# Output-product weights issued from GpSimd's queue in a two-layer hybrid attention trunk

## The chip, the cores and the metric

One core of one Trainium2 chip. The metric is the device time of one execution in microseconds; the median of several executions is given. The core's engines are TensorE (PE in the profile, its weight loads PEld), VectorE (DVE), ScalarE (ACT), GpSimd (POOL) and SyncE (SP), whose queue issues most transfers.

## The reference

Two layers over x of 256 rows and 1024 columns, and 256 rows of memory tokens, all in fp32:

```
for layer in range(2):
    h = rms_norm(x, norm_g[layer])
    sb_q, sb_k, sb_v, sb_g, mb_q, mb_k, mb_v, mb_g, mem_q, mem_g = split(h @ w_in[layer])   # 1024 x 3584
    o_sb  = stick_breaking_attention(sb_q, sb_k, sb_v) * silu(sb_g)        # 6 heads of 64
    o_mb  = causal_softmax_attention(rotary(mb_q), rotary(mb_k), mb_v) * silu(mb_g)   # 6 heads
    mk, mv = split(rms_norm(mem, mem_norm_g[layer]) @ w_mem_kv[layer])     # 1024 x 512
    o_mem = softmax_attention(mem_q, mk, mv) * silu(mem_g)                 # 4 heads
    x = x + concat(o_sb, o_mb, o_mem) @ w_out[layer]                       # 1024 x 1024
return rms_norm(x, final_norm_g)
```

With 256 rows the block-sparse attention of the reference has one block, so it is plain causal attention.

## The kernel before

**Precision.** Each weight chunk is loaded from DRAM into one of 7 buffers `raw` as fp32, then split into a high part (`hi_task`: a cast on ScalarE or VectorE) and a low part (`lo_task`: raw minus high, on VectorE); both go into one of 8 buffers `hl`. Activations are split in the same way (tiles `T`, `mxhi`, `mxlo`). Each product is three matmuls: high by high, low by high, high by low. For the pieces named in `DBL` the two with the same weights run as one 512-wide matmul and the two halves are added on VectorE afterwards.

**Chunks.** `ORDER` gives the weight pieces of each layer: column ranges of w_in, the two halves of w_mem_kv (mk, mv), and at each layer's end `wo0`, `wo1` and `wo2`, the three column ranges (384, 384 and 256) of w_out. A piece is cut into chunks of at most 768 columns by 128 rows; `KORD` is the order of w_out's eight row blocks, and only neighbouring blocks share a chunk. There are 114 chunks, 24 of them of w_out. When VectorE has made the low part of chunk j, `lo_task` issues the load of chunk j + 7 through `dma_chunk`, into the buffer that came free. All but the first two loads go out on SyncE's queue. `X_AT`, `CST_AT`, `X0_AT` and `X1_AT` say behind which chunk the transposed x, the constants and the two halves of x are loaded.

**Attention.** Head pairs of the kinds sb, mb and mem pass through `pair_scores` (matmuls on half of the array), softmax or the stick-breaking scan, `pair_turn` (32x32 transposes on VectorE into a tile `D`), a trip through DRAM, and `pair_task` (values, then the gate, then `mxhi` and `mxlo`). A trip (`trip`) is one write `Z<-D` and four reads (eight, of half the size, for the pairs in `HALVES`), into tiles shown as F, T, uT or ga. All are issued by SyncE in the same queue as the weight loads. `SCG` and `PVG` group the pairs whose scores or values go to TensorE together.

**Order.** The program is written by a planner while it is built: each stream of work is a generator, `Sched` estimates each engine's time from cost constants, and the next step is the one that can start first, by priority among steps that start within `SLACK`. All engines run their instructions in the order that comes out, each through its own queue; on a queue, an instruction that waits holds those behind it. The planner allows SyncE `RING` = 8 open transfers; it plans with the constants at the top of the file (`PRI`, the `P_` values, `HOLD`, `CROWD`, `DVE_HI` and so on). Helper lines in the profile: L261 all matmuls, L278 and L280 ScalarE's copies and activations, L284, L288, L292 and L299 VectorE's operations, L366 loads, L922 and L935 the write and reads of a trip, L486, L600 and L604 GpSimd's own DMAs (gains, and the rows of the norms).

Of the kernel before, what the change touches and what calls it, by code (L numbers as in the profile page):

```python
# [25 lines left out]
        "mem_q": (3072, 256), "mem_g": (3328, 256)}  # L26
LEAD = 8
RAW = 7
KORD = ((0, 1, 4, 5, 2, 3, 6, 7), (4, 5, 0, 1, 6, 7, 2, 3))
LAT_SAME, LAT_CROSS = 130.0, 240.0  # L30
PE_LATE = 375.1
NORM_LATE = 1029.7
DG_LATE = 885.3
COLD = 3900.0
PRI = {"sb": (-58, 4), "mb": (-198, -6), "mem": (30, 48)}
P_EV = 45
P_H0 = -22
P_RX = -136
P_M0 = 60
P_RM = -207  # L40
P_M1 = 44
URG = 1
X_AT = {4: 4, 5: 5, 8: 6, 10: 7}
CST_AT = 12
X0_AT = 15
X1_AT = 11
DMA_GBS = 330.0
RING = 8
SP_ISSUE = 450.0
POOL_ISSUE = 1000.0  # L50
# [2 lines left out]
DMA_GBS_1K = 285.0  # L53
TRIP_LAT = 1500.0
MEM_AT = 0
ORDER = (["sb_qk", "mb_k", "mb_q", "mv", "mk", "mb_g", "mem_q", "sb_v", "mb_v", "sb_g", "mem_g"], ["mv", "mk",
         "mb_q", "mb_k", "mem_q", "sb_q", "sb_k", "sb_v", "mem_g", "sb_g", "mb_g", "mb_v"])
NCH = {"sb": 3, "mb": 3, "mem": 2}
SILU = ((("sb", "mb"), ("mem",)), (("sb",), ("mb", "mem")))
TABLE = 1400.0  # L60
P_SILU = 12
SCG = (((("sb", 2), ("mem", 1), ("mb", 2)), (("mb", 1), ("mem", 0)), (("mb", 0),), (("sb", 0),), (("sb", 1),)),
       ((("mb", 0), ("sb", 2)), (("sb", 0), ("sb", 1)), (("mb", 2), ("mem", 0)), (("mem", 1),), (("mb", 1),)))
PVG = (((("mb", 1), ("mb", 0)), (("mem", 1), ("mem", 0)), (("sb", 1), ("mb", 2)), (("sb", 2),), (("sb", 0),)),
       ((("mem", 1), ("mb", 1)), (("sb", 0), ("sb", 1)), (("sb", 2), ("mb", 0)), (("mb", 2), ("mem", 0))))
HOLD = 522.1238552621808
HALVES = [("F", 0, "mem", 0), ("F", 1, "sb", 2)]
CROWD = 50
SPARE1 = 5
SPARE2 = 1  # L70
DBL = (("mb_g", 1), ("mem_g", 1), ("mk", 0), ("mk", 1), ("sb_g", 1), ("sb_k", 1), ("sb_q", 1))
DVE_W = -195.89999999999998
AHEAD = 15
DVE_HI = 1739.1999999999998
SLACK_PE = 150
SLACK = 55.400000000000006


def _free(ap):
# [22 lines left out]
class Sched:  # L102
# [63 lines left out]
    def _by_form(self, cands):  # L166
# [10 lines left out]
        for c in cands:  # L177
            f = form(c)
            if f != "full":
                first = self.held.setdefault(c[3], now)  # L180
                n = sum(form(x) == f for x in cands)
                if f == "row":
                    n = min(n, (len(self.res["bank"].items) - SPARE2) // 2)
                if n < c[3].req.get("crowd", CROWD) and now < first + HOLD:
                    continue
# [39 lines left out]
def hybrid_trunk(ctx: ExitStack, tc: tile.TileContext, x, mem, norm_g, w_in, w_mem_kv, w_out,  # L225
                 final_norm_g, xT, memT, gcols, consts, out):
    nc = tc.nc
# [3 lines left out]
    S = Sched()  # L231
# [133 lines left out]
    def dma(dst, src, name=None, q=None, now=0.0):  # L365
        (q or nc.sync).dma_start(dst, src)  # L366
        if q is None:
            S.T["sp"] = max(S.T["sp"], now, ring[-RING]) + SP_ISSUE
            now = max(now, S.T["sp"] - SP_ISSUE)
        t = queue(_free(dst) * 4 * dst.shape[0], dst.shape[-1] * 4, now)  # L370
        if q is None:
            ring.append(t)
        if name:
            S.ready[name] = t


    class Piece:
        def __init__(self, name, layer, src, width):
            self.name, self.layer, self.width, self.src = name, layer, width, src
            self.nk = CH // width  # L380
            self.kord = KORD[layer] if name[:2] == "wo" else tuple(range(KT))
            self.kmap = {}
# [7 lines left out]
    for l in range(DEPTH):  # L390
        wi = w_in[l].rearrange("(k p) c -> p k c", p=128)
        wm = w_mem_kv[l].rearrange("(k p) c -> p k c", p=128)
        wo = w_out[l].rearrange("(k p) c -> p k c", p=128)
        names = ORDER[l] + ["wo0", "wo1", "wo2"]
        for n in names:
# [27 lines left out]
    def dma_chunk(now=0.0, q=None):  # L423
        j = prog["dma"]
        if j >= len(chunks):
            return
        p, kk, c, w = chunks[j]
        n = len(kk)
        dma(raws[j % RAW][:, :n * w].rearrange("p (k c) -> p k c", c=w),
            p.src[:, kk[0]:kk[0] + n, c:c + w], ("raw", j), q, now)  # L430
        prog["dma"] += 1
        if j in X_AT:
            load_xT(X_AT[j], X_AT[j] + 1, now=now)
        for t, at in enumerate((X0_AT, X1_AT)):
            if j == at:
                dma(xs[:, t, :], x_r[:, t, :], ("x", t), now=now)
        if j == CST_AT:
            dma(cst, consts[:, 0:512], "cst", now=now)
            dma(S.res["w"].items[0][2][:, :256], consts[:, 512:768], "msk", now=now)
# [75 lines left out]
    def tr_k(p, X, c, acc, k):  # L515
        j, o = p.loc(k, c * 128)
        hi, lo = his[j % LEAD], los[j % LEAD]
        if (p.name, p.layer) in DBL:
            last = k == KT - 1
# [162 lines left out]
    def pair_scores(l, kind, c):  # L682


        group = [g for g in SCG[l] if (kind, c) in g][0]
        need = [(n, l, i) for k, i in group for n in QK[k]]
        _, sc = yield R("pe", need=["setup"] + need, alloc=["bank", "bank"],
                        spare=lambda: SPARE1 + 2 * (len(group) - 1) * (group not in begun),
                        spare2=SPARE2, form="row", crowd=CROWD if len(group) == 1 else 1)
        begun.append(group)  # L690
# [48 lines left out]
    def soft_head(l, h, kind):  # L739
# [31 lines left out]
        n = reg[1][1]  # L771
        e, _ = yield R(("act", 0.833 * n + 372.0), ("dve", 0.52 * n + 260.0 + DVE_W))
        for t, (r0, r1) in enumerate(reg):
# [27 lines left out]
    def pair_task(l, kind, c):  # L801
# [4 lines left out]
        k = HCOL[kind] // 128 + c  # L806
        group = [g for g in PVG[l] if (kind, c) in g][0]
        need = []
        for q, i in group:
            need += [("F", l, q, i), (VN[q], l)]  # L810
        _, (o,) = yield R("pe", alloc=["bank"], spare=lambda: 1 + (len(group) - 1) * ((l, group) not in begun), spare2=0,
                          form="col", crowd=1 if len(group) > 1 or kind == "mem" and c == 1 else CROWD, need=need)
        begun.append((l, group))
# [26 lines left out]
    def gate_evac(l, kind, c, acc):  # L840
        k = HCOL[kind] // 128 + c
        need = [("gm", l - 1, k)] if l else ["rx"]
        if (kind + "_g", l) in DBL:
            yield R("act", need=[n for n in need if n != "rx"])
# [20 lines left out]
    def silu_task(l, kinds):  # L865
# [7 lines left out]
        nc.scalar.preload_act_table_set("natural_log_exp_and_others")  # L873
        S.op("act", 2.0 * TABLE)
        for k in ks_:
# [42 lines left out]
    def trip(D, F, e, name, need=(), alloc=()):  # L918
# [13 lines left out]
        for j in range(4):  # L932
            for i0 in range(0, 4, 2 if name in HALVES else 4):
                i1 = i0 + (2 if name in HALVES else 4)
                nc.sync.dma_start(Fv[32 * j:32 * j + 32, i0:i1],  # L935
# [13 lines left out]
    def evac_T(l, name, c, acc, scale, rb, rneed):  # L949
        kind = {"sb_q": "sb", "sb_k": "sb", "mem_q": "mem", "mk": "mem"}[name]  # L950
        need = [("qkdone", l - 1, kind, h) for h in (2 * c, 2 * c + 1)] if l else []
        dst = (qs if name in ("sb_q", "mem_q") else ks)[kind][:, c, :]
        if ("sb_qk" if l == 0 and kind == "sb" else name, l) in DBL:
            sc = scale if rb is None else 1.0
# [79 lines left out]
    def main():  # L1034
# [7 lines left out]
        S.free("bank", acc)  # L1042
        scale_task(uT, ("xT",), 0, hT, ("h", 0), P_H0)
        for t in range(2):
            S.spawn(row_stats(2, t, xs[:, t, :], "x", rcx, rbx), P_RX)
        S.spawn(rows_done("x", "rx", rbx), P_RX)

        def mem_loads():
            load_memT(0)
            dma(gb, mem_r[:, 0, :], ("mem", 0), now=S.cur.t)  # L1050
            scale_task(uT, ("memT", 0), 16, mT, ("mT", 0), P_M0)
            S.spawn(rows_task(3, lambda t: gb, "mem", "rm", rcm, rbm), P_RM)

# [7 lines left out]
        for l in range(DEPTH):  # L1061
# [15 lines left out]
            def T_piece(n, X, nchunk, need, post):  # L1077
                p = pieces[n, l]
                for c in range(nchunk):
                    acc = yield from bank()  # L1080
                    yield from tr_unit(p, X, c, acc, need, c == nchunk - 1)
                    S.spawn(post(c, acc), P_EV, S.cur.t)

            def N_piece(n, X, need, post):
                p = pieces[n, l]
                for t in range(2):
                    acc = yield from bank()
                    yield from nat_unit(p, X, t, acc[:, :p.width], need)
                    S.spawn(post(t, acc), P_EV, S.cur.t)

# [5 lines left out]
            for kinds in SILU[l]:  # L1096
                S.spawn(silu_task(l, kinds), P_SILU)
            for h in range(SBH):
                S.spawn(scan_head(l, h), PRI["sb"][1] + h)
            for h in range(MEMH):  # L1100
                S.spawn(soft_head(l, h, "mem"), PRI["mem"][1] + h)
            for h in range(SBH):
                S.spawn(soft_head(l, h, "mb"), PRI["mb"][1] + h)
            for kind, n in (("sb", 3), ("mb", 3), ("mem", 2)):
                for c in range(n):
                    S.spawn(pair_scores(l, kind, c), PRI[kind][0] + 2)
                    S.spawn(pair_turn(l, kind, c), PRI[kind][0] + 1)
                    S.spawn(pair_task(l, kind, c), PRI[kind][0])
            if l == 0:
# [4 lines left out]
                for k in range(KT):  # L1114
                    if k < 4:
                        groups = [range(3), range(3, 6)] if k < 2 else [range(6)]
                        for g in groups:
# [3 lines left out]
                                     (los, 0, [("lo", j)])]  # L1121
                            dbl = ("sb_qk", 0) in DBL
                            if k and dbl:
# [13 lines left out]
                for c in range(6):  # L1137
                    S.spawn(evac_T(0, "sb_q" if c < 3 else "sb_k", c % 3, accs[c], 0.125 if c < 3 else 1.0, rbx, "rx"),
                            2, S.cur.t)
            for i, p in enumerate(ORDER[l]):  # L1140
                if l == 0 and i == MEM_AT:
                    mem_loads()
                if l == 0 and set(ORDER[0][i:]) <= {"mk", "mv"} and not late:
                    late.append(scale_task(uT, ("memT", 1), 24, hT, ("mT", 1), P_M1))
                if p == "sb_q" and l == 1:
# [17 lines left out]
                elif p == "mb_k":  # L1163
                    S.spawn(rope_turn(l, p), 2, S.cur.t)
                    yield from N_piece(p, hT, hneed, lambda t, acc: rope_task(
                        l, "mb_k", t, acc, rr_(t) if l == 0 else 1.0))
                if {"mk", "mv"} <= set(ORDER[l][:i + 1]) and not S.res["F%d" % l].items and l not in given:
                    given.add(l)
# [5 lines left out]
            if l == 0 and not late:  # L1174
                late.append(scale_task(uT, ("memT", 1), 24, hT, ("mT", 1), P_M1))

# [77 lines left out]
```

## Time and profile before

| | |
|---|---|
| median of 3 runs | 269.87 us (268.92 to 269.91) |
| the profiled execution | 269.51 us |
| its span, first to last instruction | 267.7 us |
| granted TensorE clock | 0.998 |
| DMA moved in all | 67.08 MB, 251 GB/s on the mean |

The span is what the rows of the profile add up to; the time of the execution is 1.8 us longer. Places in the span are given as us from its start. A row of a group of instructions names line, engine, operation, what it writes and reads (buffer numbers left out), shapes and count, then busy us and mean ns of one. A row of a wait names who waited, for whom, the sum in us, how often, and the longest.

### The profile page before, as it was taken

Reading aid. Unit: us, or ns where it says so; the run is one execution under the profiler, and the core shown is the slowest. Engines: PE = TensorE matmul, PEld = TensorE weight load, DVE = VectorE, ACT = ScalarE, POOL = GpSimd, SP = SyncE. Lnnn points to the kernel's source line nnn. Section 1 sums busy time; section 2 is a strip of 40 time slices with the busy share of each in tenths; the row PEclk is TensorE's granted clock in tenths of the full one; section 3 lists DMA queues with packets and bytes.
Section 4 is the critical chain, followed back from the end, with each engine's and each line's share of the span. In section 5 each row is a group of like instructions: output and inputs, shape, how many; then the busy total and the mean of one; then the engine's idle time right before and its main releaser. Section 6 shows DMA issues by size and latency. Waiting matters only on the chain.

```text
span 267.7 us, 5170 instructions
## 1 busy us (share of the span) xinstructions
PE 259.6 (97%) x1775; PEld 240.7 (90%) x1775; DVE 223.4 (83%) x517; ACT 187.3 (70%) x399; POOL 5.9 (2%) x18
## 2 busy tenths in 40 slices
PE   8999999999999999899999999999999999999991
PEld 4999999899999998798999999888998889989991
DVE  4696789889999999895899678689999999995382
ACT  4679888798599598771886446488778999912053
POOL 1000100200000000000000000000000000000000
PEclk9999999999999999999999999999999999999999
DMA  6999998969999899897498756857699989681004
GB/s 217 365 399 400 390 342 286 321 193 223 303 294 337 241 311 282 249 286 250 112 322 256 253 182 237 277 172 255 214 266 358 270 238 307 182 239 34 0 2 157
DMA packets 52042, 67.08 MB, mean 251 GB/s; under 512 B 4336, under 2 KB 47728, under 8 KB 52016
## 3 DMA queue, kind: packets, MB, share of 16 engines
q1 hardware_dynamic: 50928, 64.65, 77.0%
q0 software_dynamic: 512, 1.31, 1.9%
q10 hardware_dynamic: 576, 0.79, 0.9%
q8 instruction: 14, 0.23, 0.3%
q14 instruction: 12, 0.10, 0.1%
HBM read 57.29 MB, written 9.44 MB: 249 GB/s over the span
## 4 chain that ended last, share of the span: by engine, by line
PE 71%; DMA 15%; DVE 7%; ACT 3%; SPq 1%; issue 1%; DVEq 0%; ACTq 0%
PE bank L261 70%; DMA raw<-in_w_out_dram 4%; DMA raw<-in_w_in_dram 4%; DMA F<-Z 3%; DVE hl L284 2%; DMA ga<-Z 2%; DMA T<-Z 2%; ACT a L280 1%; DVE a L727 1%; DVE D L794 1%; SPq L366 1%; DVE w L292 1%; ACT hl L278 1%; PE bank L267 1%; SPq L935 1%
## 5 line engine op out<-in xcount | busy, mean ns | idle before, releaser
L284 DVE TENSOR_TENSOR hl<-raw,hl 128x768 fp32r<-128x768 f32 (+2 forms) x114 | 100.8, 897 | 10.6 <-ACT hl L278 9.7
L261 PE MATMUL bank<-T,hl 128*128 128x256 f32 (+1 forms) x720 | 106.2, 307 | 0.2 <-DVE hl L284 0.2
L261 PEld LDWEIGHTS bank<-T,hl 128*128 128x128 f32 x720 | 96.5, 190 | 8.9 <-issue 1.3
L278 ACT CAST hl<-raw 128x768 fp32r<-128x768 f32 (+2 forms) x107 | 83.0, 797 | 19.9 <-PE bank L261 11.0
L261 PE MATMUL bank<-hl,T 128*128 128x384 f32 (+1 forms) x480 | 80.2, 325 | 0.0
L261 PEld LDWEIGHTS bank<-hl,T 128*128 128x128 f32 x480 | 78.4, 188 | 0.6 <-issue 0.5
L261 PE MATMUL bank<-hl,mxhi 128*128 128x384 f32 (+1 forms) x192 | 45.5, 320 | 0.0
L261 PEld LDWEIGHTS bank<-hl,mxhi 128*128 128x128 f32 x192 | 33.3, 189 | 1.1 <-issue 1.1
L261 PE MATMUL bank<-hl,mxlo 128*128 128x384 f32 (+1 forms) x96 | 30.5, 318 | 0.0
L280 ACT ACTIVATE junk<-xs 128x384 bf16<-128x384 f32 (+2 forms) x15 | 8.0, 531 | 18.6 <-DVE xs L284 16.9
L794 DVE STREAM_TRANSPOSE D<-w 128x384 f32<-128x384 f32 (+1 forms) x32 | 19.2, 600 | 0.9 <-ACT w L280 0.9
L261 PEld LDWEIGHTS bank<-hl,mxlo 128*128 128x128 f32 x96 | 18.1, 189 | 0.2 <-DVE mxlo L284 0.2
L280 ACT ACTIVATE w<-w,st 128x256 f32<-128x256 f32 (+1 forms) x30 | 13.4, 458 | 3.6 <-DVE st L747 2.3
L727 DVE TENSOR_TENSOR_SCAN a<-a,a 128x256 f32<-128x256 f32 (+1 forms) x24 | 12.9, 538 | 1.1 <-ACT a L280 1.1
L280 ACT ACTIVATE T<-uT,gc 128x256 fp32r<-128x256 f32 x24 | 11.1, 501 | 2.1 <-DMA uT<-xT_dram 2.1
L284 DVE TENSOR_TENSOR xs<-bank,xs 128x384 f32<-128x384 f32 (+1 forms) x11 | 5.7, 520 | 7.6 <-PE bank L261 7.6
L280 ACT ACTIVATE a<-a 128x384 f32<-128x384 f32 x24 | 11.8, 525 | 0.1
L280 ACT ACTIVATE a<-bank 128x384 f32<-128x384 f32 x24 | 11.3, 485 | 0.6 <-DVE bank L284 0.5
L288 DVE SCALAR_TENSOR_TENSOR T<-uT,gc,T 128x256 fp32r<-128x256 f32 x24 | 11.4, 477 | 0.4 <-ACT T L280 0.4
L292 DVE TENSOR_SCALAR w<-w,st 128x256 f32<-128x256 f32 (+1 forms) x34 | 9.3, 317 | 0.0
L280 ACT ACTIVATE w<-bank,st 128x256 f32<-128x256 f32 x16 | 7.4, 472 | 2.8 <-DVE st L760 2.8
L284 DVE TENSOR_TENSOR ev<-bank,gT 128x256 f32<-128x256 f32 x16 | 6.4, 418 | 3.0 <-PE bank L261 3.0
(104 smaller groups left out, 211.1 us busy)
## 6 DMA issues: line engine op xcount, KB each, us to landing
raw<-in_w_in_dram SPq DMA_DIRECT2D x70, 384.0 KB, 5.1
Z<-D SPq DMA_DIRECT2D x16, 384.0 KB, 5.4
raw<-in_w_out_dram SPq DMA_DIRECT2D x16, 384.0 KB, 5.3
raw<-in_w_mem_kv_dram SPq DMA_DIRECT2D x8, 384.0 KB, 5.8
T<-Z SPq DMA_DIRECT2D x24, 96.0 KB, 4.9
uT<-memT_dram SPq DMA_DIRECT2D x8, 256.0 KB, 6.5
Z<-D SPq DMA_DIRECT2D x4, 512.0 KB, 5.9
raw<-in_w_out_dram SPq DMA_DIRECT2D x8, 256.0 KB, 3.8
```

Of the source, the lines that this page charges most:

```text
L261: nc.tensor.matmul(out, lhsT=lhsT, rhs=rhs, start=start, stop=stop, **kw)
L267: nc.tensor.transpose(out, in_, idt)
L278: nc.scalar.copy(out, in_)
L280: nc.scalar.activation(out, in_, func, **kw)
L284: nc.vector.tensor_tensor(out, a, b, op=op)
L288: nc.vector.scalar_tensor_tensor(out, a, s, b, op0=op0, op1=op1)
L292: nc.vector.tensor_scalar(out, a, s, None, op0=op)
L366: (q or nc.sync).dma_start(dst, src)
L727: nc.vector.tensor_tensor_scan(a[:, r0:r1], a[:, r0:r1], u[:, r0:r1], 0.0, OP.add, OP.add)
L794: nc.vector.transpose(o, w[:, :n * 128].rearrange("p (m j r) -> p m j r", j=4, r=32))
L935: nc.sync.dma_start(Fv[32 * j:32 * j + 32, i0:i1], Zv.rearrange("(i r) (j e) -> j r i e", i=4, j=4)[j, :, i0:i1])
```

## The change

The chunks of w_out are issued from GpSimd's queue, and the planner counts GpSimd's time for them. With it come new values of the planner's constants: the order of pieces in layer 1 and of its row blocks of w_out, the groups, priorities, the pieces in `DBL` (mem_g of layer 0 and mem_q of layer 1 are added), the places of the constants' and x's loads, and which trips are read in halves.

```
 LEAD = 8
 RAW = 7
-KORD = ((0, 1, 4, 5, 2, 3, 6, 7), (4, 5, 0, 1, 6, 7, 2, 3))
+KORD = ((0, 1, 4, 5, 2, 3, 6, 7), (0, 1, 4, 5, 6, 7, 2, 3))
...
-PRI = {"sb": (-58, 4), "mb": (-198, -6), "mem": (30, 48)}
-P_EV = 45
-P_H0 = -22
-P_RX = -136
-P_M0 = 60
-P_RM = -207
-P_M1 = 44
+PRI = {"sb": (-68, 4), "mb": (-222, -8), "mem": (-2, 18)}
+P_EV = 11
+P_H0 = -82
+P_RX = -192
+P_M0 = 38
+P_RM = -121
+P_M1 = 60
 URG = 1
-X_AT = {4: 4, 5: 5, 8: 6, 10: 7}
-CST_AT = 12
-X0_AT = 15
-X1_AT = 11
+X_AT = {5: 4, 6: 5, 7: 6, 10: 7}
+CST_AT = 6
+X0_AT = 14
+X1_AT = 13
...
-ORDER = (["sb_qk", "mb_k", "mb_q", "mv", "mk", "mb_g", "mem_q", "sb_v", "mb_v", "sb_g", "mem_g"], ["mv", "mk",
-         "mb_q", "mb_k", "mem_q", "sb_q", "sb_k", "sb_v", "mem_g", "sb_g", "mb_g", "mb_v"])
+ORDER = (["sb_qk", "mb_k", "mb_q", "mv", "mk", "mb_g", "mem_q", "sb_v", "mb_v", "sb_g", "mem_g"], ["mk", "mv",
+         "mb_q", "mb_k", "mem_q", "sb_k", "sb_q", "sb_v", "mem_g", "sb_g", "mb_g", "mb_v"])
...
-TABLE = 1400.0
-P_SILU = 12
-SCG = (((("sb", 2), ("mem", 1), ("mb", 2)), (("mb", 1), ("mem", 0)), (("mb", 0),), (("sb", 0),), (("sb", 1),)),
-       ((("mb", 0), ("sb", 2)), (("sb", 0), ("sb", 1)), (("mb", 2), ("mem", 0)), (("mem", 1),), (("mb", 1),)))
-PVG = (((("mb", 1), ("mb", 0)), (("mem", 1), ("mem", 0)), (("sb", 1), ("mb", 2)), (("sb", 2),), (("sb", 0),)),
-       ((("mem", 1), ("mb", 1)), (("sb", 0), ("sb", 1)), (("sb", 2), ("mb", 0)), (("mb", 2), ("mem", 0))))
-HOLD = 522.1238552621808
-HALVES = [("F", 0, "mem", 0), ("F", 1, "sb", 2)]
-CROWD = 50
+TABLE = 1290.0
+P_SILU = 16
+SCG = (((("sb", 1),), (("mem", 0), ("mb", 0), ("mb", 2)), (("sb", 2), ("mem", 1)), (("mb", 1),), (("sb", 0),)),
+       ((("mb", 0), ("sb", 2)), (("sb", 1), ("sb", 0)), (("mb", 1), ("mem", 1)), (("mb", 2),), (("mem", 0),)))
+PVG = (((("mem", 0), ("mem", 1)), (("sb", 1), ("mb", 2)), (("mb", 1), ("mb", 0)), (("sb", 2),), (("sb", 0),)),
+       ((("sb", 0), ("sb", 1)), (("sb", 2),), (("mem", 1), ("mb", 2), ("mem", 0), ("mb", 1)), (("mb", 0),)))
+HOLD = 652.654819077726
+HALVES = [("F", 0, "mem", 0), ("F", 0, "mem", 1)]
+CROWD = 46
 SPARE1 = 5
-SPARE2 = 1
-DBL = (("mb_g", 1), ("mem_g", 1), ("mk", 0), ("mk", 1), ("sb_g", 1), ("sb_k", 1), ("sb_q", 1))
-DVE_W = -195.89999999999998
-AHEAD = 15
-DVE_HI = 1739.1999999999998
-SLACK_PE = 150
-SLACK = 55.400000000000006
+SPARE2 = 0
+DBL = (("mb_g", 1), ("mem_g", 0), ("mem_g", 1), ("mem_q", 1), ("mk", 0), ("mk", 1), ("sb_g", 1), ("sb_k", 1),
+       ("sb_q", 1))
+DVE_W = -295.9
+AHEAD = 20
+DVE_HI = 1339.1999999999998
+SLACK_PE = 20
+SLACK = 65.4
...
         p, kk, c, w = chunks[j]
         n = len(kk)
+        if p.name[:2] == "wo":
+            q = nc.gpsimd
+            S.T["pool"] = max(S.T["pool"], now) + POOL_ISSUE
+            now = S.T["pool"]
         dma(raws[j % RAW][:, :n * w].rearrange("p (k c) -> p k c", c=w),
             p.src[:, kk[0]:kk[0] + n, c:c + w], ("raw", j), q, now)
```

## Prediction

> **What bounds the kernel now.** I read the page's first table, then the waits of TensorE, then busy time by stretches, then the chain that ended last.
>
> ```profile
> span 267.7 us, 5170 instructions
> PE 259.6 (97%) x1775; PEld 240.7 (90%) x1775; DVE 223.4 (83%) x517; ACT 187.3 (70%) x399; POOL 5.9 (2%) x18
> ```
>
> ```profile
> PE bank L261 <- DMA F<-Z: 1.0, 1, 1.0
> PE bank L261 <- DMA T<-Z: 0.3, 1, 0.3
> PE bank L261 <- DVE hl L284: 0.2, 1, 0.2
> ```
>
> TensorE is busy 259.6 of 267.7 us and idles behind other work for 1.5 us in all (besides the start of the program, before anything is loaded). So waits can give 1.5 us and no more; anything further must come out of TensorE's own instructions. Where the 1.5 us lies, the stretches show (busy us of PE, PEld, DVE, ACT, POOL in turn, instructions in brackets):
>
> ```profile
> 70.00:80.00 10.00, 10.00 (x72) 9.25 (x72) 10.00 (x44) 7.81 (x28) 0.00 (x0) 1.00 0.94 281
> 80.00:90.00 10.00, 10.00 (x67) 9.26 (x67) 10.00 (x23) 9.23 (x20) 0.00 (x0) 1.00 1.00 316
> 90.00:100.00 10.00, 10.00 (x86) 9.30 (x84) 9.10 (x27) 6.87 (x22) 0.00 (x0) 1.00 0.94 278
> 100.00:110.00 10.00, 8.76 (x79) 7.59 (x77) 9.57 (x25) 7.44 (x9) 0.00 (x0) 1.00 1.02 281
> 110.00:120.00 10.00, 10.00 (x62) 9.51 (x58) 9.44 (x18) 8.29 (x14) 0.00 (x0) 1.00 0.94 265
> ```
>
> TensorE loses 1.24 us between 100 and 110 us, the end of layer 0's attention. VectorE is nearly as full there: its idle time from 70 to 120 us is 0.90 + 0.43 + 0.56 = 1.9 us. So this stretch has two bounds, and TensorE's gap can close only as far as VectorE follows. The chain says what ended the gap:
>
> ```profile
> 97.86 5.54 DMA raw<-in_w_out_dram
> ...
> 104.25 5.25 DMA F<-Z
> 109.50 0.14 issue
> 109.64 28.08 PE bank L261 x189
> ...
> 145.52 116.71 PE bank L261 x751
> ```
>
> A w_out load (5.54 us) stands ahead of the read F<-Z (5.25 us) that TensorE waits for at 109.64. Behind that the chain is TensorE to its last matmul, 145.52 + 116.71 = 262.2 us: layer 1 has no wait, so nothing to gain there by queues. How the load comes to stand before the read is seen in SyncE's queue, its waits from 84 to 112 us and its issues:
>
> ```profile
> SPq L366 <- DVE hl L284: 4.7, 3, 2.0
> SPq L935 <- DMA raw<-in_w_out_dram: 3.6, 4, 1.5
> ```
>
> ```profile
> 95.62 0.41 SPq L922 DMA_DIRECT2D Z<-D  x1
> 97.86 0.38 SPq L366 DMA_DIRECT2D raw<-in_w_out_dram  x1
> 98.29 1.88 SPq L935 DMA_DIRECT2D T<-Z  x4
> 100.27 0.38 SPq L922 DMA_DIRECT2D Z<-D  x1
> 101.67 0.39 SPq L366 DMA_DIRECT2D raw<-in_w_out_dram  x1
> 102.15 2.53 SPq L935 DMA_DIRECT2D F<-Z  x4
> ```
>
> First, SyncE stands 4.7 us before loads into raw until VectorE's subtraction frees a buffer, and everything queued behind stands too. Second, four reads of a trip stood 3.6 us until an earlier w_out load had landed, though they use nothing of it: SyncE keeps a limited number of transfers open (RING, 8 in the code).
>
> **The change part by part.**
>
> *The queue.* 24 loads (16 of 384 KB and 8 of 256 KB before; after it layer 1's third piece splits as 2, 3, 1 and 2 row blocks, so still 24) leave SyncE for GpSimd, 12 in each layer.
>
> ```profile
> L366 SPq DMA_DIRECT2D raw<-in_w_out_dram x24: 367/389/415, 83.7 to 234.8; - x24
> raw<-in_w_out_dram SPq DMA_DIRECT2D x16, 384.0 KB, 5.3
> Z<-D SPq DMA_DIRECT2D x16, 384.0 KB, 5.4
> gb<-in_norm_g_dram POOLq DMA_DIRECT2D x1, 512.0 KB, 7.4
> gb<-in_final_norm_g_dram POOLq DMA_DIRECT2D x1, 512.0 KB, 5.2
> ACT hl L278 <- DMA raw<-in_w_out_dram: 2.8, 2, 1.8
> L600 POOL DMA_DIRECT2D rows_x<-rt x2 | 1.3, 638 | 8.3 <-DVE rt L596 8.3
> ```
>
> SyncE saves 12 x 0.389 = 4.7 us of issue in each layer. Where it counts: the write to DRAM at 95.62 has landed at about 95.62 + 5.4 = 101.0, and the reads F<-Z began at 102.15. Without the load at 101.67 and its wait they could begin at 101.0, 1.1 us earlier, and take 1.88 instead of 2.53 us, 0.6 us less: 1.7 us, more than the 1.0 us that TensorE waited. The T<-Z read before it (0.3 us of waiting) stood behind the load at 97.86 in the same way: SyncE was free at 95.62 + 0.41 = 96.0, and that load held it for 1.8 us. I take both waits away: **-1.3 us**, with ends 0 (VectorE holds TensorE back all the same) and -1.3.
>
> GpSimd pays 24 issues. The nearest row is 0.64 us for one of its own small DMAs; the loads name twice the rows of any GpSimd DMA in the trace, so I allow 0.6 to 1.3 us each, 14 to 31 us. GpSimd is busy 5.9 of 267.7 us, and its eight other DMAs stand outside the two groups of 12 in its program order: the cover is idle time. A load that waits for its buffer on GpSimd has only w_out loads behind it. What is late next is the load itself: GpSimd's 512 KB took 5.2 and 7.4 us to land, SyncE's 384 KB 5.3, so a load lands between 0.1 us earlier and 2 us later. Before, ScalarE's casts waited for such a load twice, 2.8 us in all, and TensorE for none of it; so I cost it at **0**, hidden by the casts' lead over TensorE, and keep +1 as an end, the half of the later landing that a cast without lead would pass on.
>
> *GpSimd beside VectorE.* In the tight stretch, 84 to 118 us, VectorE runs these instructions with one source and one target, both in SBUF:
>
> ```profile
> L292 DVE TENSOR_SCALAR w<-w,st 128x256 f32<-128x256 f32 x7 | 2.2, 344 | 0.0
> L299 DVE CAST mxhi<-ev 128x256 fp32r<-128x256 f32 x4 | 1.0, 283 | 0.0
> L299 DVE CAST hl<-raw 128x768 fp32r<-128x768 f32 x1 | 0.5, 540 | 0.0
> ```
>
> That is 12 instructions and 3.7 us of 34. Twelve issues of 0.64 us are 7.7 us, 23% of the stretch. If an issue can hold such an instruction, 12 x 0.23 = 3 are met, for 0.3 us each: 0.8 us, under VectorE's 1.9 us of idle time. I take **0**, ends 0 and the full 7.7 us. The Trainium skill (SBUF — State Buffer, the box on the "DVE blocks DMA" trap) speaks against the change: a DMA issued from GpSimd can't write its descriptors while VectorE holds the shared pair of ports in a two-port mode. By that rule each load starts at most one such instruction, 0.54 us, later, and the sum stays; its reverse, VectorE waiting for GpSimd, is a rival below. No row of before shows such a pair meeting. The skill (DMA: Bandwidth & Descriptors, Issuing engines are not separate DMA queues) also says that another queue saves only the issuer's time, usually little; by that this would be 4.7 us of issue off a queue that is not the bound, and no change at all. The two SyncE rows above differ from it: the larger price was waiting in order.
>
> *Doubled pieces.* mem_g of layer 0 and mem_q of layer 1 join DBL: per row block and 128 columns one 512-wide and one 256-wide matmul in place of three of 256, 16 such sets each, 32 in all.
>
> ```profile
> 61.72 4.48 PE L261 MATMUL bank<-T,hl 128*128 128x256 f32 x36
> 202.21 22.79 PE L261 MATMUL bank<-T,hl 128*128 128x512 f32 x128
> L284 DVE TENSOR_TENSOR gT<-bank,rbx 128x256 f32<-128x256 f32 x5 | 2.0, 407 | 0.4 <-PE bank L261 0.4
> ```
>
> Three of the first row take 4.48 / 12 = 0.373 us (0.36 without the last one's tail), a pair of the second 22.79 / 64 = 0.356. That is 0.004 to 0.017 us a set, 0.1 to 0.5 us: **-0.3 us**. It costs VectorE an addition (0.407 us) for each of 2 + 2 chunks; in layer 0 that is 0.8 us in the stretch where VectorE has 1.9 us free.
>
> *The start.* The constants (256 + 128 KB) come behind chunk 6 and not chunk 12, xT's blocks 4 and 5 one chunk later, x's halves behind chunks 13 and 14.
>
> ```profile
> 6.33 6.04 DMA raw<-in_w_in_dram
> 14.50:22.50 8.00, 8.00 (x68) 1.00 1.06 401
> ```
>
> Chunk 6, issued at 6.33, ends TensorE's 0.2 us wait. 128 KB less stand before it: at 401 GB/s 0.3 us earlier, which covers that wait: **-0.2 us**. Chunk 7 and what follows get 384 KB in front, 1.0 us later; TensorE takes 4.48 / 2 = 2.2 us for a chunk of the first piece (18 matmuls) while one lands every 1.0 us, so each next chunk has 1.2 us more in hand. Ends -0.2 and +0.5 for chunk 7.
>
> *Order, priorities, groups.* Still 5 groups of scores in each layer, 5 and 4 of values; the same matmuls, in new places; four more split reads of Z in layer 0, four fewer in layer 1, for HALVES. Which instruction stands where can't be read from the trace of before. Nearest rows: layer 1's chain without any wait (+0) and one trip's read, 5.25 us, as the longest wait that one mistimed group could bring. I take **0** and keep -1.5 (fewer changes of TensorE's array form) to +5.
>
> Sum: -1.3 - 0.3 - 0.2 = -1.8 us. The profiled execution took 269.51 us (span 267.7), so 267.7; it lies 0.36 us under the median of 269.87, so as a median **268.1**.
>
> **Rivals.**
>
> 1. *VectorE is the real bound of the stretch* and the trips' earlier landing is hidden. For it: 10.00 of 10 us busy from 70 to 90 us, and 0.8 us of additions put in. Against: 1.9 us free up to 120 us. Then only -0.3 - 0.2 remain: 269.4.
>
> 2. *GpSimd's issues hold VectorE.* Place: the 12 loads at 84 to 118 us. Price: up to 7.7 us of VectorE's time; beyond the 1.9 us free it delays the subtractions that TensorE consumes, and beyond 1.9 + 1.8 = 3.7 us, six full holds, the kernel is slower than before. All twelve: 267.7 + 7.7 - 1.9 + 0.36 = 273.9; eight, 5.1 us: 271.3. Against: only 3 of 12 are likely to meet. The skill's page on SBUF calls the shared pair an exclusive lock for the whole instruction, which would make this price whole where it is met.
>
> 3. *A group in the new order waits for its last member*, with the values of layer 1's group of four the likeliest place: TensorE then has only output product left to fill in. Half of a 5.25 us read is 2.6 us: 270.7. For it: before had no wait there, so a new place can only lose. It decides from 1.8 us on.
>
> 4. *The groups meet better* and TensorE changes form less often: a further -1.5 us, 266.6. The page can't show it.
>
> **How the numbers follow.** Chances: forecast 0.42, rival 1 0.22, rival 2 0.08, rival 3 0.18, rival 4 0.10. About 0.5% is what a measurement of this kernel can tell from no change: 268.5 and 271.2 are the borders. Faster: 0.85 of the forecast, whose end at 268.1 lies close to the border, rival 4 and a little of rival 1: 0.48. Slower: half of rival 3, rival 2 and the tails: 0.21. Same: 0.31. The range holds rival 4 below, 266.4, and reaches to 271.6 above, past rival 3 and the smaller price of rival 2, leaving out its full price and a lone mistimed group of 5 us. The forecast's own range is 267.3 to 269.0.
>
> **What would show it.** Right: no wait of TensorE for F<-Z or T<-Z between 95 and 115 us; no row of SyncE waiting for a w_out load; GpSimd with 24 issues more, each under 1.3 us; TensorE's last matmul near 260.4 us. Wrong on GpSimd: one-source instructions of VectorE longer than 344, 283 and 540 ns while an issue runs, or loads landing over 8 us after it. Wrong on the start: a wait for chunk 7 near 16 us. Wrong on the order: a new row of TensorE waiting behind 145 us, or more changes of form. Rival 1 would show the gap near 108 us again, ended by VectorE.

## The result, and the profile after

The changed kernel takes 272.25 us (median of 4 runs, 271.54 to 272.72) where the kernel before takes 269.57 on the same chip (4 runs): a ratio of 1.010, 95% interval 1.0068 to 1.0132. It is slower by 2.7 us; 268.1 was forecast, with 271.6 as the upper end. Three executions below lie far above the others of their kernel (427.26 us of e6, 274.32 of e9 and 272.82 of e10, the last two at a granted clock of 0.989 and 0.990): the medians count them, the ratios do not. The profiled execution took 272.38 us, 2.87 more than the one before.

First the page, its head and its row of the granted clock (one digit for a fortieth of the span, 6.8 us):

```profile
span 270.6 us, 5144 instructions
PE 260.9 (96%) x1743; PEld 239.6 (89%) x1743; DVE 225.4 (83%) x525; ACT 185.6 (69%) x397; POOL 23.5 (9%) x42
...
PEclk9999999999999999799999999999999999999997
```

TensorE is busy 260.9 us, 1.3 more than before, though the change took 32 matmuls away. The clock row has the reason: a 7 in the seventeenth slice, 108 to 115 us. The time is again lost at the end of layer 0's attention. The waits of TensorE in the whole run (the second row is the start of the program):

```profile
PE bank L262 <- DMA T<-Z: 2.6, 1, 2.6
PE bank L262 <- DVE junk L1042: 1.2, 1, 1.2
```

And the same stretches as before, with three shorter ones around the wait (us, then busy us of PE, PEld, DVE, ACT, POOL; then clock, DMA share, GB/s):

```profile
100.00:110.00 10.00, 7.70 (x58) 5.75 (x54) 9.76 (x27) 7.39 (x9) 2.13 (x3) 1.00 0.98 305
110.00:120.00 10.00, 9.56 (x47) 8.35 (x48) 6.32 (x11) 6.83 (x13) 2.13 (x3) 0.83 0.53 154
120.00:200.00 80.00, 80.00 (x523) 73.74 (x523) 68.49 (x163) 48.62 (x110) 0.55 (x1) 1.00 0.74 229
```

```profile
104.00:107.31 3.31, 3.31 (x26) 2.67 (x22) 3.31 (x11) 2.32 (x4) 1.03 (x2) 1.00 1.02 326
107.31:110.00 2.69, 0.39 (x3) 0.07 (x1) 2.45 (x9) 1.10 (x2) 0.00 (x0) 1.00 0.92 280
110.00:113.41 3.41, 3.08 (x13) 2.46 (x14) 1.29 (x2) 0.82 (x2) 0.00 (x0) 0.50 0.37 109
```

This is the whole account. From 100 to 120 us TensorE idles 2.30 + 0.44 = 2.7 us, where before it idled 1.24: +1.5. Behind the wait it runs at half its clock for 3.41 us and is busy for 3.08 of them, which costs half of the 3.08: +1.5. The rest of the program is 0.1 us shorter. Together +2.9, the difference of the spans. From 120 us on TensorE never waits.

What is late? The transfers of the stretch, by tile (engine, count, size of one, median us from issue to landing), from 95 to 112 us, before and then after:

```profile
raw<-in_w_out_dram SPq DMA_DIRECT2D x4, 384.0 KB, 5.5
...
T<-Z SPq DMA_DIRECT2D x8, 64.0 KB, 4.1
...
F<-Z SPq DMA_DIRECT2D x4, 96.0 KB, 5.2
```

```profile
raw<-in_w_out_dram POOLq DMA_DIRECT2D x3, 384.0 KB, 6.8
...
T<-Z SPq DMA_DIRECT2D x8, 64.0 KB, 5.9
F<-Z SPq DMA_DIRECT2D x4, 96.0 KB, 7.3
```

SyncE did what was foreseen. Its queue in the changed kernel:

```profile
99.11 0.34 SPq L927 DMA_DIRECT2D Z<-D  x1
101.06 1.76 SPq L940 DMA_DIRECT2D F<-Z  x4
103.71 0.34 SPq L927 DMA_DIRECT2D Z<-D  x1
```

The F<-Z reads begin at 101.06 instead of 102.15 and take 1.76 us. But they land 7.3 us after issue, the last at 110.19 where before it was 109.50: issued up to 1.9 us earlier, landed 0.7 us later. The waits view names T<-Z for TensorE's 2.6 us, but the matmuls that begin then, at 110.33, read F; they follow the last F read by 0.14 us, as before.

A second transfer is late. The chain that ended last passes through a load of w_out:

```profile
103.61 8.90 DMA raw<-in_w_out_dram
...
112.59 0.66 ACT hl L279
...
113.33 1.31 ACT T L281 x3
114.64 0.30 ACT mxhi L279
...
114.99 0.45 PE bank L262
```

This is the load of chunk 53, the eighth of layer 0's w_out: 8.90 us, where before it took 5.41 on SyncE's queue. ScalarE executes in order. It stands at the cast of this chunk (its `hl`), and behind it, in its program, stand three activations into T and the cast `mxhi`, for which TensorE waits. ScalarE's waits from 104 to 118 us, before and after:

```profile
ACT hl L278 <- DMA raw<-in_w_out_dram: 2.8, 2, 1.8
```

```profile
ACT hl L279 <- DMA raw<-in_w_out_dram: 4.8, 2, 4.1
...
```

This first profile is not the rule. In c_after_again, the same kernel once more, the last F read lands at 107.42 us, 2.1 us earlier than before, and TensorE idles 0.23 us from 100 to 110 us. Its row of the four reads, and then what TensorE waits for, `mxhi` behind ScalarE:

```profile
F<-Z SPq DMA_DIRECT2D x4, 96.0 KB, 5.7
```

```profile
PE bank L262 <- ACT mxhi L279: 1.4, 1, 1.4
```

### The profile page after: what moved, and what is told of

The parts are those of the page before. It is cut to its first block, busy times and chain, and to the rows that moved or that the text cites. A ratio compares the mean times of both kernels' runs of the same rounds, so it can differ in the third digit from the quotient of the medians.

```text
span 270.6 us, 5144 instructions
## 1 busy us (share of the span) xinstructions
PE 260.9 (96%) x1743; PEld 239.6 (89%) x1743; DVE 225.4 (83%) x525; ACT 185.6 (69%) x397; POOL 23.5 (9%) x42
## 4 chain that ended last, share of the span: by engine, by line
PE 89%; DMA 4%; DVE 3%; ACT 1%; issue 1%; SPq 0%; DVEq 0%; POOLq 0%; ACTq 0%
PE bank L262 88%; DMA raw<-in_w_out_dram 3%; DMA uT<-xT_dram 1%; DVE hl L285 1%; ACT T L281 1%; PE bank L268 1%; DVE w L293 1%; DVE D L799 0%; DVE w L752 0%; ACT hl L279 0%; ACT ss L281 0%; ACT junk L281 0%; DVE hl L300 0%; SPq L367 0%; DVE xs L293 0%
## 5 line engine op out<-in xcount | busy, mean ns | idle before, releaser
L285 DVE TENSOR_TENSOR hl<-raw,hl 128x768 fp32r<-128x768 f32 (+3 forms) x114 | 100.4, 895 | 11.3 <-ACT hl L279 10.6
L262 PEld LDWEIGHTS bank<-T,hl 128*128 128x128 f32 x688 | 94.6, 190 | 9.6 <-issue 1.7
L262 PE MATMUL bank<-hl,mxhi 128*128 128x384 f32 (+1 forms) x192 | 46.1, 323 | 0.1
L367 POOL DMA_DIRECT2D raw<-in_w_out_dram x24 | 17.0, 708 | 133.2 <-DMA raw<-in_w_in_dram 68.3
L281 ACT ACTIVATE w<-w,st 128x256 f32<-128x256 f32 (+1 forms) x26 | 11.6, 450 | 5.5 <-DVE st L752 5.0
L293 DVE TENSOR_SCALAR w<-w,st 128x256 f32<-128x256 f32 (+1 forms) x38 | 10.5, 321 | 0.0
```

Source lines behind the costliest of these rows:

```text
L262: nc.tensor.matmul(out, lhsT=lhsT, rhs=rhs, start=start, stop=stop, **kw)
L281: nc.scalar.activation(out, in_, func, **kw)
L285: nc.vector.tensor_tensor(out, a, b, op=op)
L293: nc.vector.tensor_scalar(out, a, s, None, op0=op)
```

## The experiments

All kernels but e2 keep the changed kernel's order. e1 to e3 and e5 to e10 change only the queue that w_out's loads are issued from; e4 adds matmuls, e11 and e12 cut the loads, and c_after_again and c2_after_third are the changed kernel again. Where the queue changes, `dma` gets one more argument, and `dma_chunk` passes it; the planner's own account of the queues stays as it is, so that every engine's program stays in the same order:

```diff
-    def dma(dst, src, name=None, q=None, now=0.0):
-        (q or nc.sync).dma_start(dst, src)
+    def dma(dst, src, name=None, q=None, now=0.0, on=None):
+        (on or q or nc.sync).dma_start(dst, src)
```

In the expectations theory A is that the loads' queue is what costs, and theory B that the new order and groups do; A1 is that any second queue would do it, A2 that it is GpSimd's. What each kernel measured, with two readings of its one profile: TensorE's idle time from 100 to 120 us (from the stretches) and the time from the issue of chunk 53's load to its landing. A ratio is taken against the executions of the kernel before in the same series (medians 268.98 to 269.57), so it is not the quotient of two rows.

| kernel | w_out loads of layer 0 | median us | ratio to before, 95% | TensorE idle, 100 to 120 | chunk 53, us to land |
|---|---|---|---|---|---|
| before | SyncE | 269.57 | 1 | 1.24 | 5.4 |
| changed | GpSimd | 272.25 | 1.010, 1.0068 to 1.0132 | 2.74 | 8.9 |
| c_after_again | GpSimd | 270.48 | 1.0066, 1.0033 to 1.0099 | 1.63 | 6.8 |
| c2_after_third | GpSimd | 271.85 | 1.0088, 1.0059 to 1.0116 | 2.14 | 7.3 |
| e1 | SyncE (layer 1 too) | 268.87 | 0.9986, 0.9966 to 1.0007 | 0.71 | 6.0 |
| e2 | GpSimd, old order | 270.44 | 1.0041, 1.0018 to 1.0064 | 1.84 | 7.8 |
| e3 | SyncE | 269.26 | 1.0001, 0.9974 to 1.0028 | 0.24 | 5.4 |
| e4 | GpSimd, gap filled | 271.02 | 1.0081, 1.0052 to 1.0111 | 0.11 (filled) | 7.4 |
| e5 | ScalarE (layer 1 too) | 275.44 | 1.0221, 1.0174 to 1.0267 | 3.93 | 6.0 |
| e6 | GpSimd, chunks 52 and 53 SyncE | 268.36 | 0.9963, 0.9942 to 0.9984 | 0.22 | 5.2 |
| e10 (e6 again) | the same | 268.67 | 0.9982, 0.9969 to 0.9996 | 0.28 | 5.3 |
| e7 | SyncE, chunks 52 and 53 GpSimd | 269.75 | 1.0020, 0.9994 to 1.0046 | 1.38 | 5.9 |
| e8 | GpSimd, chunk 53 SyncE | 269.26 | 1.0010, 0.9995 to 1.0025 | 0.32 | 5.2 |
| e9 | GpSimd, chunk 52 SyncE | 270.09 | 1.0040, 1.0018 to 1.0062 | 1.49 | 6.6 |
| e11 | GpSimd, row blocks apart | 270.46 | 1.0041, 1.0021 to 1.0061 | 1.49 | 6.5 |
| e12 | GpSimd, partitions apart | 271.72 | 1.0100, 1.0072 to 1.0129 | 1.94 | 7.0 |

**Queue or order (e1, e2, e3).** The edits, in `dma_chunk`:

```diff
 e1 (changed kernel):  + q, on = nc.gpsimd, nc.sync
 e2 (kernel before):   + on = nc.gpsimd if p.name[:2] == "wo" else None
 e3 (changed kernel):  + q, on = nc.gpsimd, nc.gpsimd if p.layer else nc.sync
```

> The changed kernel in its new order, with all 24 w_out loads issued from SyncE again at the same places of the program. Theory A (two queues share the saturated DMA engines, so the read F<-Z lands later; the longer gap of TensorE then halves its clock for 3.4 us): the four reads land 5 to 6 us after issue instead of 7.8, the gap before the last values of layer 0 is under 1.6 us, no half clock, 269.3 us (268.6 to 270.0). Theory B (the new order is at fault): as changed, 271.5 to 272.7. Theory C (GpSimd's issues hold VectorE): 269.3 as well, but with VectorE's one-source instructions shorter than in the changed kernel.

> The kernel before in its old order, with the 24 w_out loads issued from GpSimd at the same places. Theory A: reads of trips between 90 and 112 us land 6.5 to 9 us after issue, a gap of 2 to 3 us before the last values of layer 0 and a half clock behind it, 271 to 273 us. Theory B: the waits in SyncE's queue go and nothing else: 268.2 to 269.5.

> The changed kernel with layer 0's 12 w_out loads on SyncE and layer 1's 12 on GpSimd. Theory A: all of the loss is made in layer 0, so as with all loads on SyncE within 0.5 us: 269.3 (268.6 to 270.0). If layer 1's loads cost too: 270.5 or more. Theory B: 271.5 to 272.7.

The new order with all loads on SyncE runs like the kernel before (0.9986, the interval holds 1); the old order with the loads on GpSimd is slower by 0.4%. So the order alone costs nothing, and the queue does. Whether the new order makes the queue's price larger (1.0066 to 1.010 against e2's 1.0041) isn't settled: the intervals of e2 and c_after_again overlap. Layer 1's loads may go to GpSimd at no cost that shows (e3, 1.0001, within 0.3%): the loss is in layer 0. In e2's profile the wait is there without the new order, and it is the one behind ScalarE:

```profile
ACT hl L278 <- DMA raw<-in_w_out_dram: 4.0, 2, 2.0
...
PE bank L261 <- ACT mxhi L278: 1.8, 1, 1.8
```

**The clock (e4, and the changed kernel again).** Twelve matmuls of a tile that nobody reads, ahead of the values that wait for F:

```diff
+        if (l, kind, c) == (0, "sb", 2):
+            for _ in range(12):
+                nc.tensor.matmul(o, lhsT=junk[:, :128], rhs=junk[:, :512], start=True, stop=True)
```

> The changed kernel with 12 bf16 matmuls on a constant tile, into the bank that the values overwrite, ahead of the last values of layer 0: they fill TensorE's gap of 2.7 us and change nothing else. If the half clock behind the gap comes of the gap itself, and costs 1.7 us: no half clock after 110 us, 270.5 us (270.0 to 271.0). If the clock falls for another reason: as changed, 272.2, with half clock in the same place.

> The changed kernel once more, beside the kernels that are compared with it. By both theories 271.5 to 272.7 us, the four reads F<-Z issued near 101 us land 6.5 to 8 us after issue, TensorE's gap before the last values of layer 0 is 2 to 3 us, and in some executions its clock is halved behind the gap.

In none of e4's 10 runs was the granted clock under 0.994, against 0.987 in the profile above; but the twelve matmuls take 2.6 us (at 0.216 each) also where F lands in time (at 107.86 us in its profile), so nothing is won: 271.02, where 270.0 to 271.0 was expected. Three of the ten took 272.3 to 273.4 us without a low clock, so a long run is not always the clock's; what made those long isn't shown. The changed kernel's own runs show what the clock is worth. In its three series (c_after_again came out under the 271.5 to 272.7 that was expected) it ran 23 times: 11 times at a granted clock of 0.990 or less, median 272.4 us, and 12 times above, median 270.4. The kernel before was at or under 0.991 in none of its 105 runs beside the experiments. So the waits cost some 1.3 us (270.4 against 269.1, the median of the 105), and in about half of the runs the clock falls as well, for 2.0 more. The profile of c2_after_third, one of those, shows it in another place:

```profile
108.00:110.58 2.58, 2.35 (x16) 1.69 (x13) 2.58 (x7) 0.00 (x0) 0.00 (x0) 1.00 0.96 232
110.58:113.99 3.41, 1.49 (x7) 0.92 (x6) 1.01 (x3) 3.24 (x8) 0.71 (x1) 1.00 0.49 157
113.99:117.40 3.41, 3.41 (x13) 3.41 (x12) 3.41 (x7) 1.61 (x4) 1.42 (x2) 0.50 0.49 166
```

```profile
PE bank L262 <- ACT mxhi L279: 1.9, 1, 1.9
```

Here no single wait is longer than the 1.9 us of the second fence, TensorE's waits from 95 to 120 us (for `mxhi`, behind ScalarE), but TensorE is busy for only 1.49 of the 3.41 us ahead of the drop; in the first profile it was 1.11 of 3.41 (0.72 + 0.39), with a longest gap of 2.6 us. The length of a gap alone doesn't decide: in e5's profile one of 2.3 us made no drop. Both drops last 3.41 us. The Trainium skill (TensorE: Matmul & The Clock Gate, What's actually happening) gives a free-running window of 3413 ns and half the clock behind an idle one: the length agrees; but a window in which TensorE was busy for 33 or 44% was enough here.

ScalarE's wait ahead of its cast of chunk 53 is put down to an instruction of VectorE in this profile. But the load landed at 110.67 us and the cast began at 110.75, and in e6 the same cast began 1.6 us ahead of that instruction (108.79 and 110.35), so it doesn't need it: here too it is the load.

**A second hardware queue (e5).**

```diff
+            q, on = nc.gpsimd, nc.scalar
```

> The changed kernel in its new order with the w_out loads on ScalarE's queue: again a second queue beside SyncE's, but not GpSimd's. ScalarE will stand while a load waits for its buffer, so its time says little; what counts is how the reads of trips land between 84 and 112 us. Theory A1 (any second queue shares the saturated DMA engines, and more transfers are open): median issue to landing 6 us or more. Theory A2 (GpSimd's queue alone makes some DMA engines late): under 5.3 us, and the last of the 16 DMA engines within 0.5 us of the 14th.

As a kernel it is the worst: ScalarE now stands at a load until its buffer is free, and its activations with it (its waits for VectorE's low parts are 3.8 us from 84 to 118 us, and none in the changed kernel). As a measurement it separates the queues. The same transfers, 95 to 112 us:

```profile
raw<-in_w_out_dram ACTq DMA_DIRECT2D x3, 384.0 KB, 5.2
...
F<-Z SPq DMA_DIRECT2D x4, 96.0 KB, 5.3
...
T<-Z SPq DMA_DIRECT2D x6, 64.0 KB, 3.1
```

With a second queue that is not GpSimd's nothing of this lands late. That speaks for A2 (GpSimd's queue), with one reservation: ScalarE's standing also moved the loads apart in time.

**Which loads (e6, e7, then e8, e9, e10).** Chunks 52 and 53 are issued among the reads of Z that TensorE waits for, at 100.5 and 103.6 us.

```diff
 e6, e10:  + q, on = nc.gpsimd, nc.sync if j in (52, 53) else nc.gpsimd
 e7:       + q, on = nc.gpsimd, nc.gpsimd if j in (52, 53) else nc.sync
 e8:       + q, on = nc.gpsimd, nc.sync if j == 53 else nc.gpsimd
 e9:       + q, on = nc.gpsimd, nc.sync if j == 52 else nc.gpsimd
```

> The changed kernel with two of layer 0's w_out loads on SyncE again, those in flight beside the reads F<-Z (the loads of chunks 52 and 53). If those two loads make the reads late: reads land within 6 us, the gap is under 1.7 us, 269.5 us. If the backlog comes of all the loads before: reads land 6.5 us or more after issue, 271.5 us.

> The opposite: all w_out loads on SyncE but the two of chunks 52 and 53, which stay on GpSimd. If those two make the reads late: a gap of 2 us or more, 271 us or more. If the backlog of the earlier loads does: as with all loads on SyncE, 269.0 us (268.4 to 269.6).

Two loads of 24 are enough to end the loss. With them alone back on SyncE's queue (e6) the kernel beats the one before and the changed one: 268.36 us, 0.9963. They are not enough to make it: with them alone on GpSimd's (e7) the four F<-Z reads take 6.8 us (median) and TensorE idles 1.38 us until 0.13 us behind the last of them, but chunk 53 lands in 5.9 us, and at 1.0020 the interval just holds 1. Its 269.75 us lie between what the two theories of e7 said (271 or more; 269.0), and by this one profile chunk 53 is late only with more of the loads on GpSimd's queue. SyncE's queue in e6 and the wait that TensorE has left there (95 to 125 us):

```profile
100.44 0.40 SPq L367 DMA_DIRECT2D raw<-in_w_out_dram  x1
100.94 2.11 SPq L941 DMA_DIRECT2D F<-Z  x4
103.46 0.40 SPq L367 DMA_DIRECT2D raw<-in_w_out_dram  x1
```

```profile
PE bank L262 <- DVE mxlo L285: 0.2, 1, 0.2
```

Two loads cost SyncE 0.40 us each, and the F<-Z reads still begin 1.2 us earlier than before.

> The changed kernel with one load of layer 0 alone, chunk 53's, back on SyncE's queue; the other 23 stay on GpSimd's, chunk 52's too. With 52 and 53 both on SyncE it took 268.36 us, with all on GpSimd 270.48 and 272.25. Theory L (what costs is the late landing of chunk 53, for which ScalarE stands in order, with the maximum's cast that TensorE waits for behind it): nearly the whole gain comes from this one load, 268.2 to 268.9, chunk 53 lands within 6 us of its issue and no wait of TensorE near 114 us. Theory R (what costs is the late reads F<-Z and T<-Z, which share the DMA engines with the loads of chunks 52 and 53): chunk 52 (issued near 100.5, landed near 107) still shares with them, so half of the gain at most, 269.3 to 270.5, with TensorE's gap near 107.5 still over 1 us.

> The other way round: chunk 52's load alone back on SyncE's queue, chunk 53's and the other 22 on GpSimd's. Theory L: no gain from it, 270.0 to 272, chunk 53 lands 6.5 to 9 us after its issue, ScalarE stands 2 to 5 us for it and TensorE over 1 us for the maximum's cast. Theory R: half of the gain, 269.3 to 270.0, since chunk 52's packets stand ahead of the reads that TensorE waits for.

> The version with the loads of chunks 52 and 53 on SyncE's queue and the other 22 on GpSimd's, again, on this call's chip, as the measure for the two beside it and to see whether it beats the kernel before a second time. If it does for the reason given (reads early, no late load), 268.0 to 268.7 and a ratio under 0.998; if the first time was the chip's, 269.0 to 269.5.

The profiles side with L. Against 1.0066 to 1.010 for the changed kernel, chunk 53 alone brings it to 1.0010 and chunk 52 alone to 1.0040, both together to 0.9982 (e10; 0.9963 the first time, both intervals under 1). The larger part is chunk 53's, as L had it. In e8 the gap that R asked for (over 1 us near 107.5) isn't there, TensorE idles 0.32 us from 100 to 120 us, and in e9 all that L named came: 270.09 us, 6.57 us to land, ScalarE standing 2.1 and TensorE 1.2 us. Two things are left over: e8's 269.26 lies over L's 268.9, and e9's 1.0040 is less than the changed kernel's ratios, though not clear of 1.0066. The reads of Z are as late in the good kernels as in the bad: issued from 84 to 112 us they take 4.8 us in the middle before, 6.6, 5.8 and 5.7 in the three profiles of the changed kernel, and 6.0, 5.6 and 5.7 in e6, e8 and e10, where TensorE waits for none of them longer than 0.1 us. Why 53 is the larger part stands in the waits of ScalarE, 104 to 118 us, in e8 and then in e9, and what TensorE waits for in e9:

```profile
ACT hl L279 <- DMA raw<-in_w_out_dram: 0.6, 2, 0.5
```

```profile
ACT hl L279 <- DMA raw<-in_w_out_dram: 2.1, 1, 2.1
```

```profile
PE bank L262 <- ACT mxhi L279: 1.2, 1, 1.2
```

```profile
103.29 6.57 DMA raw<-in_w_out_dram
...
109.94 0.84 ACT hl L279
110.78 0.94 ACT T L281 x3
...
111.89 0.40 ACT mxhi L279
```

In e9 chunk 53 lands after 6.57 us, the cast begins 0.08 us behind it, and everything in line behind the cast is late by as much. With chunk 53 on SyncE's queue that row is gone from TensorE's waits.

**Why transfers land late (e11, e12, c2_after_third).** The page's table of queues (packets, MB, share of 16 engines) in e1 and in the changed kernel:

```profile
q1 hardware_dynamic: 50928, 64.65, 75.8%
q0 software_dynamic: 512, 1.31, 1.8%
```

```profile
q1 hardware_dynamic: 44400, 56.26, 64.7%
q0 software_dynamic: 2944, 9.70, 12.5%
```

8.39 MB moved from SyncE's queue (q1) to GpSimd's (q0): 6528 packets there, 1.29 KB each on the mean, become 2432 here, 3.45 KB each. The Trainium skill (DMA: Bandwidth & Descriptors, Queues, rings and completion order) says that each engine takes turns between queues by whole packets; by that, if its packets are those of the table, larger packets take more of an engine that is full, and the stretch is full (DMA share 1.02). e11 and e12 were to test this, with as many transfers, cut so as to make packets small or not:

```diff
+        for k in range(parts):                          # e11, one per row block
+            q.dma_start(dst[:, k], src[:, k])
+        for k in range(parts):                          # e12, by partitions
+            a, b = 128 * k // parts, 128 * (k + 1) // parts
+            q.dma_start(dst[a:b], src[a:b])
```

> The changed kernel, each load of w_out in layer 0 issued from GpSimd's queue as one transfer for each row block (3 or 4 for one), so that a packet should carry one row block's 1536 or 1024 bytes of a partition, as on SyncE's queue, and not 4608 or 4096. Theory S (the large packets: where the DMA engines are full, each of GpSimd's takes 257 ns beside 45 to 90 of SyncE's, so GpSimd's queue gets more than its share and the reads of Z wait): the reads of Z issued from 84 to 112 us land in 4.8 to 5.4 us in the middle (changed kernel 6.6, before 4.8), and the time is 268.4 to 269.7. Theory Q (GpSimd's queue itself, whatever the size): the reads stay at 5.8 to 6.8 us, the time at 270 to 272.5 or above, since each load is also issued later by 1.4 us or more.

> The control for the run beside it: as many transfers for each load of layer 0 on GpSimd's queue, but cut by partitions, so that a packet still carries all row blocks of a partition, 4608 or 4096 bytes. Theory S: reads of Z still at 5.8 to 6.8 us in the middle, time 270 to 273. Theory Q: the same. If it runs as fast as the one cut by row blocks, then it is the spacing of the issues that helps and not the packets' size.

> The changed kernel once more on this call's chip, as the measure for the two beside it: 270.3 to 272.3, reads of Z from 84 to 112 us at 5.8 to 6.6 us in the middle.

e11 missed its aim: a load of these has two row blocks and not three or four, and GpSimd's queue put its rows together again across partitions: a transfer of one row block has at most 1.5 KB in a partition, and the packets stay larger. Its row of the page, the same in packets and MB for e12:

```profile
q0 software_dynamic: 3136, 9.70, 11.6%
```

That is 3.2 KB a packet on the mean, little less than 3.45. Still e11 is the faster one (1.0041 against 1.0100 and 1.0088), its F<-Z reads took 4.7 us in the middle and e12's 6.1, and two of its 12 runs had the clock at 0.990 (two of e12's 6 at 0.988 and 0.989). The intervals of e11 and e12 don't touch, so the difference in time is more than noise; with packets of one size it can't be theirs, and with one profile each its cause isn't shown. So it stays open why the transfers land late: the packets' size, loads standing behind each other in GpSimd's queue, VectorE holding up GpSimd's part of a load, or something else of that queue; no packet of the small size could be had on it here.

## Why the prediction was wrong, by its own steps

*SyncE's queue, -1.3.* The half on issues was right: F<-Z from 101.06 (foreseen 101.0) in 1.76 us (1.88), no row of SyncE waiting for a w_out load. What was carried over in silence is the reads' 5.25 us to land, from a trace in which GpSimd's queue was empty. In the first profile it became 7.3 us, and of the 1.7 us gained on issue none reached TensorE. In the two repeats it was 5.7 and 5.3 us, the last F read landed at 107.42 and 107.13 us (before: 109.50), and TensorE waited for none: there this term held, and its gain was lost again behind ScalarE. How much of it is the queue's isn't shown either: in e3, with layer 0's loads on SyncE's queue, the new order alone brings TensorE's idle time to 0.24 us (0.71 in e1).

*GpSimd's loads, 0.* The issues were priced right (0.6 to 1.3 us) and are hidden:

```profile
L367 POOL DMA_DIRECT2D raw<-in_w_out_dram x24 | 17.0, 708 | 133.2 <-DMA raw<-in_w_in_dram 68.3
```

The loads' landing is the step that failed, in all three profiles of the changed kernel. Its range, to 2 us later, came from the right rows and holds e9's 6.57, c_after_again's 6.80 and c2_after_third's 7.30 against 5.41 us, though not the first profile's 8.90. The mistake was the zero: TensorE "for none of it". ScalarE had waited 2.8 us for two such loads before, so its cast had no lead to hide anything; the whole lateness, and not half of it, passed to what stood behind the cast, with TensorE at the end: it waited 1.4 and 1.9 us for `mxhi` in the two repeats, 1.8 in e2 and 1.2 in e9. The row was quoted, and what stood behind ScalarE's wait was not looked up.

*The clock.* Not a term at all: 1.5 us in the profile, and a drop in about half of the runs. The trace of before had gaps of 0.3 and 1.0 us without a drop, and no row said how much more it would bear.

*GpSimd beside VectorE, 0.* Held. VectorE's one-source instructions from 84 to 118 us in the changed kernel:

```profile
L293 DVE TENSOR_SCALAR w<-w,st 128x256 f32<-128x256 f32 x7 | 2.2, 350 | 0.0
...
L300 DVE CAST mxhi<-ev 128x256 fp32r<-128x256 f32 x5 | 1.5, 322 | 0.0
L300 DVE CAST hl<-raw 128x768 fp32r<-128x768 f32 x1 | 0.5, 541 | 0.0
```

350, 322 and 541 ns against 344, 283 and 540: 0.2 us in all at most (in e1, without GpSimd's issues, the second is 280). Rival 2 (271.3 to 273.9) came near in time by luck and is not the cause.

*Doubled pieces, start, order: -0.5 together.* e1 holds just these: 0.9986, interval 0.9966 to 1.0007, that is -0.9 to +0.2 us. It fits and can't be told from nothing. TensorE's 0.2 us wait at the start is gone in the changed kernel (e1 has one of 0.2 again). The -0.3 of the doubled pieces doesn't show: with 32 matmuls fewer TensorE is busy 259.6 us in e1, as before, and 259.5 in e3 and e10.

*Rivals.* 3 (a group of layer 1 that waits): no, TensorE is busy for 80.00 of the 80 us behind 120, and its list of waits has none behind that. 1 (VectorE the real bound): in part; where transfers are in time the last wait is VectorE's, 0.6 us in e1 and 0.2 in e6. The prediction's list of what would show it wrong did name loads that land over 8 us after issue, but gave that no time.

## What to carry to other kernels

A landing time read from a trace holds for the traffic of that trace: here, with the DMA engines full, moving 12 loads to GpSimd's queue changed how long they and the reads beside them took, and a step that only makes an issue earlier must say what it takes the landing to be. Where an engine in order already waits for a transfer, that transfer has no slack, and every us that it lands later is paid by all that stands behind the wait. Move the transfers that have slack, and leave the two or three that are awaited, and are issued among others that are awaited, on the queue where they land soonest (here 22 of 24 moved: 268.4 to 268.7 us, ratio 0.9963 and 0.9982). That moving the 22 wins anything isn't shown: e1, which moves none, took 268.9 us (0.9986), and the intervals overlap.

## What the runs showed of the hardware

- Loads issued from GpSimd go in packets of 3.45 KB on the mean where the same loads from SyncE go in 1.29 KB, and rows of different partitions share a packet. While the engines were full the load of chunk 53 took 6.5 to 8.9 us from GpSimd's queue with others there, 5.2 to 6.0 from SyncE's and 6.0 from ScalarE's. The reads on SyncE's queue landed later too (F<-Z 5.2 to 7.3 us, T<-Z 4.1 to 5.9 in the first profile; 5.7 and 5.3, 5.8 and 5.4 in the repeats); in layer 1 no cost showed (e3).
- The Trainium skill (DMA: Bandwidth & Descriptors, Issuing engines are not separate DMA queues), by which another queue saves only the issuer's time, is not the whole of it: two loads issued from one engine or the other changed the kernel by 1.0% (1.0066 against 0.9963 on one chip, 1.0088 against 0.9982 on two).
- The clock of TensorE halves for 3.41 us behind 3.41 us in which it was busy a third to under a half of the time, with no single gap over 2.6 us in one case and 1.9 in the other.
